# Twenty-five transposes of a two-layer encoder trunk, moved from TensorE to VectorE and a round trip through DRAM

## The chip, the cores and the metric

The kernel runs on one core of a Trainium2 chip. The metric is the device time of one execution in microseconds (us). Before the change the median of three runs is 2019.36 us (2019.31 to 2019.63).

## What is computed

Two layers act on x (256 tokens by 2048 channels, float32). Each layer normalises x and multiplies it by one wide matrix; the result feeds three token mixers and their gates. The outputs of the mixers are gated, projected to 2048 channels, scaled by sigmoid gates, summed, and sent through one more matrix into the residual. Cut to what matters here:

```python
h = _rmsnorm(x, g_pre)
u = h @ w_in                                       # 2048 -> 16192 columns
o_a = _mla_attention(qn, qr, kn, kr, v)            # A: low-rank q and kv
o_b = _rmsnorm(_diff_attention(bq, bk, bv, lam), b_g_sub) * (1.0 - lam_init)
cq = _rmsnorm(c_q.reshape(b, s, C_HEADS, C_DH), c_g_q)
ck = _rmsnorm(c_k.reshape(b, s, C_HEADS, C_DH), c_g_k)
o_c = _chunk_band_attention(cq, ck, cv, c_rel_bias)
branches = (o_a * silu(a_z), o_b * silu(b_z), o_c * silu(c_z))
y = sum(gates[:, :, n] * (branches[n] @ w_branch[n]) for n in range(3))
x = x + y @ w_out                                  # then the next layer
```

## The kernel before

All large products are weight streams. `matunit` computes a 256 x 512 block of a product (two PSUM tiles of 128 tokens) from chunks of weights: 256 rows by 512 columns, 512 KB each. For each chunk SyncE's queue loads it (L153, `_r`), ScalarE rounds it to float32r (L154, `_h`), VectorE forms the remainder (L155, `_l`), and TensorE runs twelve matmuls of 512 columns on it: two row blocks of the chunk, two token tiles, and three products each (high by high L163, remainder by high L164, high by low L165). Four chunks can be loaded ahead (`wrp`), three pairs can stand ready (`wsp`). A block over 2048 rows is a "unit" of 8 chunks, one over 1024 rows has 4.

A layer goes through its units in the order of `stream_plan`: cq, ckv and branch A; branch B in two halves of four heads (k, q, v, z); the first gate branch (n = 0: for each of four column blocks j one gate unit of 8 chunks and one branch unit of 4); branch C in two halves; the gate branches n = 1 and n = 2; the output projection in four column blocks (`l0o`), whose results are also the next layer's x.

Activations are computed with tokens on the partitions. The next product needs them with channels on the partitions. `to_transposed` (L199) does this: TensorE multiplies each 128 x 128 block by the identity (L205) into a PSUM tile, eight such transposes for 256 x 512 values, and ScalarE and VectorE split the tile into a high and a low part (`split`, L168, its lines L174 and L175). It is called for q and k of every branch, for z of A and C in `simple_half` (L352), for B's results in `b_split` (L546), for the four column blocks of y at the end of gate branch 2 (L639), and for the four column blocks of the next x (L702).

The code is written unit by unit. The order on each engine is made by a scheduler that runs the program through a model of time; each engine then works through its own list in order, and so does SyncE's queue of DMA issues.

Of the kernel before, what the change touches and what calls it, by code (L numbers as in the profile page):

```python
# [8 lines left out]
F32 = mybir.dt.float32  # L9
# [5 lines left out]
P = 128  # L15
# [6 lines left out]
HH = 4  # L22
# [20 lines left out]
def stream_plan():  # L43

    order = []
    for l in range(DEPTH):
# [35 lines left out]
def trunk_kernel(ctx: ExitStack, tc: tile.TileContext, x, xT, w, cols, rows, tab, bias, ident_d, out):  # L82
# [10 lines left out]
    natp = ctx.enter_context(tc.tile_pool(name="natp", bufs=6))  # L93
# [42 lines left out]
    state = {"off": 0}  # L136

    def matunit(lhs, K, N, name, pre=None):
# [3 lines left out]
        for c in range(nk // 2):  # L142
# [8 lines left out]
            for ks in ((slice(0, 1), slice(1, 2)) if o == 0 else (slice(0, 2),)):  # L151
                if o:
# [3 lines left out]
                                        op=ALU.subtract)  # L156
            for k2 in range(2):
# [56 lines left out]

    def rstd(ss, n, width, name):
# [4 lines left out]
    def qk_natural(ps, gs, rcol, name):  # L220

        ng = 512 // gs
        nats = [natp.tile([P, 512], F32, tag="nat", name=f"{name}_n{t}") for t in range(NT)]
# [19 lines left out]
        return nats  # L243
# [108 lines left out]
    def simple_half(z, parts, v, add, name):  # L352

        zt = zp.tile([P, HH, SEQ], F32, tag="z", name=f"{name}zt")
        to_transposed(lambda t: z[:, t, :], HH, None, None, None, f"{name}zT",
                      put=lambda bs, pt: nc.scalar.copy(zt[:, bs, :], pt))
        for hl in range(HH):
# [10 lines left out]
            nc.vector.tensor_tensor(out=zt[:, hl, :], in0=o[:, :SEQ], in1=zt[:, hl, :], op=ALU.mult)  # L368
# [39 lines left out]
    for l in range(DEPTH):  # L408
# [84 lines left out]
        ncq = []  # L493
        for t in range(NT):
# [4 lines left out]
            nat = natp.tile([P, 512], F32, tag="nat", name=f"ncq{l}{t}")  # L499
            nc.scalar.activation(nat, pcq[t], AF.Copy, scale=ss[:, t:t + 1])  # L500
            ncq.append(nat)
        abig = bigp.tile([P, 4, HH, SEQ], F32R, tag="big", name=f"abig{l}")
        cqh, cql = abig[:, 0], abig[:, 1]
        to_transposed(lambda t: ncq[t], 4, cqh, cql, lambda b: gcol(G_CQ + b), f"cqT{l}", per_block=True)
# [4 lines left out]
        nkv = []  # L509
        for t in range(NT):  # L510
# [9 lines left out]
            nat = natp.tile([P, 512], F32, tag="nat", name=f"nkv{l}{t}")  # L520
# [6 lines left out]
            nkv.append(nat)  # L527
# [18 lines left out]
        def b_split(z, hf, name, gain=None):  # L546
            bh[hf] = zp.tile([P, HH, SEQ], F32R, tag=f"bh{hf}", name=f"{name}h", bufs=1)
            bl[hf] = zp.tile([P, HH, SEQ], F32R, tag=f"bl{hf}", name=f"{name}l", bufs=1)
            if gain is None:
                split(bh[hf], bl[hf], z)  # L550
            else:
                to_transposed(lambda t: z[:, t, :], HH, bh[hf], bl[hf], gain, name)
# [229 lines left out]
```

## Time and profile before

| | |
|---|---|
| median of three runs | 2019.36 us |
| the profiled execution | 2019.73 us |
| its span, first to last instruction | 2018.0 us |
| granted TensorE clock, mean | 1.00 of full speed |
| TensorE busy | 2008.6 us, 100% |
| VectorE busy | 1228.0 us, 61% |
| ScalarE busy | 1117.8 us, 55% |
| moved by DMA | 377.37 MB, 187 GB/s over the span |

In the profile PE is TensorE, PEld its weight loads (they overlap with matmuls), DVE VectorE, ACT ScalarE, POOL GpSimd, SPq SyncE's queue of DMA issues. Names like `l0c0k` read as layer 0, branch C, half 0, k; `l0n2j1b` as layer 0, gate branch 2, column block 1, branch product; `l0g` are the gate units, `l0o` the output projection. L205 is line 205 of the kernel before. The chain of waits follows the instruction that ended last back to what released it at each step; an instruction in it lasts there from the end of the one before, not as long as its own record.

### The profile page before, as it was taken

To read this page: it belongs to the slowest core of one execution; us is meant where nothing else is said; L and a number is where in the kernel's file an instruction comes from. 1 tells how busy PE (TensorE), PEld (TensorE's weight loads), DVE (VectorE), ACT (ScalarE), POOL (GpSimd) and SP (SyncE) were. 2 spreads that over 40 slices of the span, in tenths; PEclk is the share of its full clock that TensorE was granted. 3 is DMA by queue.
4 is the path that set the end of the run, shared out by engine and by line. 5 is a ranking of instruction groups with operands and counts; after the bars stand their busy time and mean duration, and the time that the engine had idled before them with its cause. 6 is when DMAs were issued, how large, how long until landed. Compare 5 with 4: busy or idle time off the path is not lost.

```text
span 2018.0 us, 25748 instructions
## 1 busy us (share of the span) xinstructions
PE 2008.6 (100%) x9448; PEld 1676.6 (83%) x9448; DVE 1228.0 (61%) x1686; ACT 1117.8 (55%) x1658; POOL 218.6 (11%) x357
## 2 busy tenths in 40 slices
PE   9999999999999999999999999999999999999999
PEld 7888888888888888888888888888888888888887
DVE  5777878545555555555557778775455655555554
ACT  6666767445565544445456767674456555444443
POOL 2313040001000000000023130400010100000000
PEclk9999999999999999999999999999999999999999
DMA  8554545566555556557665445555665555565565
GB/s 288 185 165 151 175 165 184 180 206 193 185 170 184 173 193 194 191 186 242 208 191 181 157 157 176 168 169 189 206 199 178 167 187 175 192 196 189 188 240 156
DMA packets 107183, 377.37 MB, mean 187 GB/s; under 512 B 11937, under 2 KB 16033, under 8 KB 106289
## 3 DMA queue, kind: packets, MB, share of 16 engines
q1 hardware_dynamic: 104848, 366.75, 55.6%
q0 software_dynamic: 1920, 8.46, 1.4%
q8 instruction: 74, 1.21, 0.3%
q14 instruction: 53, 0.43, 0.1%
q10 hardware_dynamic: 288, 0.52, 0.1%
HBM read 371.49 MB, written 4.19 MB: 186 GB/s over the span
## 4 chain that ended last, share of the span: by engine, by line
PE 98%; DMA 1%; ACT 0%; DVE 0%; SPq 0%; issue 0%; ACTq 0%
PE l0g_p L164 4%; PE l1g_p L164 4%; PE l1g_p L165 4%; PE l0g_p L165 4%; PE l1g_p L163 4%; PE l0g_p L163 4%; PE l0o_p L163 1%; PE l0o_p L164 1%; PE l0o_p L165 1%; PE l1o_p L165 1%; PE l1o_p L163 1%; PE l1o_p L164 1%; DMA l0cq_r<-w 1%; PE l0az_p L164 1%; PE l0az_p L163 1%; PE l1az_p L164 1%
## 5 line engine op out<-in xcount | busy, mean ns | idle before, releaser
L155 DVE TENSOR_TENSOR l0g_l<-l0g_r,l0g_h 128x1024 fp32r<-128x1024 f32 x96 | 117.5, 1224 | 109.6 <-ACT l0g_h L154 109.6
L155 DVE TENSOR_TENSOR l1g_l<-l1g_r,l1g_h 128x1024 fp32r<-128x1024 f32 x96 | 117.5, 1225 | 109.6 <-ACT l1g_h L154 109.6
L154 ACT CAST l0g_h<-l0g_r 128x1024 fp32r<-128x1024 f32 x96 | 101.1, 1053 | 136.3 <-PE l0g_p L165 85.6
L154 ACT CAST l1g_h<-l1g_r 128x1024 fp32r<-128x1024 f32 x96 | 101.1, 1053 | 136.0 <-PE l1g_p L165 85.6
L164 PE MATMUL l1g_p<-l1g_l,xh 128*128 128x512 f32 x384 | 150.3, 391 | 0.0
L164 PE MATMUL l0g_p<-l0g_l,xh 128*128 128x512 f32 x384 | 150.3, 391 | 0.0
L165 PE MATMUL l1g_p<-l1g_h,xl 128*128 128x512 f32 x384 | 149.9, 390 | 0.0
L165 PE MATMUL l0g_p<-l0g_h,xl 128*128 128x512 f32 x384 | 149.9, 390 | 0.0
L163 PE MATMUL l0g_p<-l0g_h,xh 128*128 128x512 f32 x384 | 136.3, 391 | 0.0
L163 PE MATMUL l1g_p<-l1g_h,xh 128*128 128x512 f32 x384 | 136.3, 391 | 0.0
L163 PEld LDWEIGHTS l0g_p<-l0g_h,xh 128*128 128x128 f32 x384 | 72.0, 188 | 14.8
L164 PEld LDWEIGHTS l0g_p<-l0g_l,xh 128*128 128x128 f32 x384 | 72.1, 188 | 14.7
L164 PEld LDWEIGHTS l1g_p<-l1g_l,xh 128*128 128x128 f32 x384 | 72.1, 188 | 14.7
L163 PEld LDWEIGHTS l1g_p<-l1g_h,xh 128*128 128x128 f32 x384 | 72.0, 188 | 14.8
L165 PEld LDWEIGHTS l1g_p<-l1g_h,xl 128*128 128x128 f32 x384 | 72.1, 188 | 14.5
L165 PEld LDWEIGHTS l0g_p<-l0g_h,xl 128*128 128x128 f32 x384 | 72.1, 188 | 14.5
L155 DVE TENSOR_TENSOR l1o_l<-l1o_r,l1o_h 128x1024 fp32r<-128x1024 f32 x32 | 39.2, 1225 | 41.6 <-ACT l1o_h L154 41.6
L154 ACT CAST l1o_h<-l1o_r 128x1024 fp32r<-128x1024 f32 x32 | 33.8, 1055 | 53.2 <-PE l1o_p L165 48.2
L155 DVE TENSOR_TENSOR l0o_l<-l0o_r,l0o_h 128x1024 fp32r<-128x1024 f32 x32 | 39.2, 1225 | 36.1 <-ACT l0o_h L154 36.0
L154 ACT CAST l0o_h<-l0o_r 128x1024 fp32r<-128x1024 f32 x32 | 33.7, 1054 | 40.9 <-PE l0o_p L165 31.2
L680 POOL DMA_DIRECT2D xres<-xscr x1 | 0.8, 792 | 315.7 <-PE l1n2j3yT_t L205 315.7
L680 POOL DMA_DIRECT2D xres<-x x1 | 0.8, 784 | 315.7 <-PE l0n2j3yT_t L205 315.7
(1646 smaller groups left out, 5904.4 us busy)
## 6 DMA issues: line engine op xcount, KB each, us to landing
l0g_r<-w SPq DMA_DIRECT2D x96, 512.0 KB, 3.4
l1g_r<-w SPq DMA_DIRECT2D x96, 512.0 KB, 3.4
l0o_r<-w SPq DMA_DIRECT2D x32, 512.0 KB, 4.2
l1o_r<-w SPq DMA_DIRECT2D x32, 512.0 KB, 4.2
l0az_r<-w SPq DMA_DIRECT2D x16, 512.0 KB, 3.6
l1az_r<-w SPq DMA_DIRECT2D x16, 512.0 KB, 3.7
l0b0k_r<-w SPq DMA_DIRECT2D x8, 512.0 KB, 3.3
l0b0q_r<-w SPq DMA_DIRECT2D x8, 512.0 KB, 3.4
```

Of the source, the lines that this page charges most:

```text
L154: state["cast"] = nc.scalar.copy(wh[:, ks, :N], wr[:, ks, :N])
L155: nc.vector.tensor_tensor(out=wl[:, ks, :N], in0=wr[:, ks, :N], in1=wh[:, ks, :N].bitcast(F32), op=ALU.subtract)
L163: nc.tensor.matmul(ps[t][:, :N], h[:, ts], wh[:, k2, :N], start=first, stop=False)
L164: nc.tensor.matmul(ps[t][:, :N], h[:, ts], wl[:, k2, :N], start=False, stop=False)
L165: nc.tensor.matmul(ps[t][:, :N], lo[:, ts], wh[:, k2, :N], start=False, stop=last)
L680: nc.gpsimd.dma_start(xres, x_src.rearrange("(t p) d -> p t d", p=P))
```

## The change

For 25 of the blocks of 256 x 512 values `to_transposed` gives way to a new helper, `bounce`. VectorE transposes each 128 x 512 tile in squares of 32 x 32 (`nc.vector.transpose`, two instructions per block) into a tile `_tu`; SyncE's queue writes that tile to a scratch area in DRAM (`_scr`, 512 KB in runs of 2 KB); four more DMAs read it back with the squares in their transposed places, each 32 partitions of eight runs of 512 bytes. The read brings the values into the tile they came from, or into another one (`dst`). `from_bounced` then splits them from SBUF into high and low parts. The 25 are: in each layer k, q and z of both halves of C, the results of both halves of B, and y's column blocks 0 to 2; and once the next x's column blocks 0 to 2. Column block 3 of y and of x, all of A, and B's k and q stay with TensorE.

The steps of a trip are spaced by weight chunks: `later(n, fn)` runs `fn` when n more chunks have been issued, and `issue_after` keeps a write or a read behind that chunk's load on SyncE's queue and a split behind that chunk's cast on ScalarE. For C's k and q the write comes after 8, the read after 10, the two halves of the split after 12 and 13 chunks; for C's z 6 and 8; for B 28 and 30; for y 9, 11 and 13; for x 7, 9 and 11. In C the unit of z now comes before that of v. The two gate activations of a unit run with the second token tile first (`gates`). The tiles of normalised q and k are allocated as pairs (`natp`, 3 of twice the size where there were 6). The multiplication with C's gate reads and writes z in the order in which the trip left it (`bounced`, `as_bounced`).

```diff
-            for s in (1, 0, 2, 3):
+            for s in (1, 0, 3, 2):
                 win("c", qc + s * BW + hf * 512, 512)
...
-    natp = ctx.enter_context(tc.tile_pool(name="natp", bufs=6))
+    natp = ctx.enter_context(tc.tile_pool(name="natp", bufs=3))
...
-    state = {"off": 0}
+    state = {"off": 0, "n": 0}
+    due = []
+    away = set()
+    def later(n, fn):
+        due.append((state["n"] + n, fn))
+    def run_due():
+        state["n"] += 1
+        for x in [x for x in due if x[0] <= state["n"]]:
+            due.remove(x)
+            x[1]()
...
+            run_due()
...
+    def nat_pair(name):
+        return natp.tile([P, NT, 512], F32, tag="nat", name=name)
+    def bounce(src, name, at, then=None, dst=None):
+        turned = zp.tile([P, NT, 4, HH, 32], F32, tag="z", name=f"{name}_tu")
+        scr = dram.tile([NT, P, 4, 128], F32, name=f"{name}_scr")
+        for t in range(NT):
+            nc.vector.transpose(turned[:, t].rearrange("p j b c -> p b j c"), src[:, t, :])
+        dst = src if dst is None else dst
+        flat = dst.rearrange("p t f -> p (t f)")
+        away.add(name)
+        def write():
+            with tc.issue_after(state["last"].ins):
+                nc.sync.dma_start(scr.rearrange("t p j f -> p t (j f)"), turned.rearrange("p t j b c -> p t (j b c)"))
+        def read():
+            sv = scr.rearrange("t (i r) j f -> j r (t i) f", r=32)
+            with tc.issue_after(state["last"].ins):
+                for j in range(4):
+                    nc.sync.dma_start(flat[32 * j:32 * j + 32].rearrange("p (q f) -> p q f", f=128), sv[j])
+            if then is None:
+                away.remove(name)
+        def use(b0):
+            with tc.issue_after(state["cast"].ins):
+                then(flat, slice(b0, b0 + 2))
+            if b0:
+                away.remove(name)
+        later(at[0], write)
+        later(at[1], read)
+        if then is not None:
+            later(at[2], lambda: use(0))
+            later(at[2] + 1, lambda: use(2))
+        return flat
+    def bounced(z, b):
+        return z.rearrange("p (q b c) -> p q b c", b=HH, c=32)[:, :, b, :]
...
+    def as_bounced(d):
+        if len(d.shape) == 2:
+            return d.rearrange("p (q c) -> p q c", c=32)
+        return d.rearrange("p b (q c) -> p q b c", c=32)
+    def from_bounced(z, bs, dh, dl, gain):
+        if gain is None:
+            split(as_bounced(dh[:, bs, :]), as_bounced(dl[:, bs, :]), bounced(z, bs))
+        else:
+            one = not callable(gain)
+            if one:
+                nc.scalar.activation(as_bounced(dh[:, bs, :]), bounced(z, bs), AF.Copy, scale=gain)
+            for b in range(bs.start, bs.stop):
+                g = gain if one else gain(b)
+                h, lo, zb = as_bounced(dh[:, b, :]), as_bounced(dl[:, b, :]), bounced(z, b)
+                if not one:
+                    nc.scalar.activation(h, zb, AF.Copy, scale=g)
+                nc.vector.scalar_tensor_tensor(out=lo, in0=zb, scalar=g, in1=h.bitcast(F32),
+                                               op0=ALU.mult, op1=ALU.subtract)
...
+    def gates(z, ps, rcol, func):
+        i = nc.scalar.activation(z[:, 1, :], ps[1], func, scale=rcol[:, 1:2])
+        with tc.issue_after(i.ins):
+            nc.scalar.activation(z[:, 0, :], ps[0], func, scale=rcol[:, 0:1])
     def silu_gate(ps, rcol, name):
         z = zp.tile([P, NT, 512], F32, tag="z", name=name)
-        for t in range(NT):
-            nc.scalar.activation(z[:, t, :], ps[t], AF.Silu, scale=rcol[:, t:t + 1])
+        gates(z, ps, rcol, AF.Silu)
...
-    def simple_half(z, parts, v, add, name):
-        zt = zp.tile([P, HH, SEQ], F32, tag="z", name=f"{name}zt")
-        to_transposed(lambda t: z[:, t, :], HH, None, None, None, f"{name}zT",
-                      put=lambda bs, pt: nc.scalar.copy(zt[:, bs, :], pt))
+    def simple_half(zt, block, view, parts, v, add, name):
...
-            nc.vector.tensor_tensor(out=zt[:, hl, :], in0=o[:, :SEQ], in1=zt[:, hl, :], op=ALU.mult)
+            zc = block(hl)
+            nc.vector.tensor_tensor(out=zc, in0=view(o[:, :SEQ]), in1=zc, op=ALU.mult)
...
+            for b0 in (0, 2):
+                from_bounced(z, slice(b0, b0 + 2), bh[hf], bl[hf], gain)
...
+            zb[hf] = bounce(zb[hf], f"{n}bT", (28, 30))
...
-                    to_transposed(lambda t: yacc[:, t, js], 4, yh[j], yl[j], None, f"{nm}yT")
+                    if j < 3:
+                        yz = zp.tile([P, NT, 512], F32, tag="z", name=f"{nm}yz")
+                        bounce(yacc[:, :, js], f"{nm}yT", (9, 11, 13),
+                               lambda z, bs, yt=yt: from_bounced(z, bs, yt[:, 0], yt[:, 1], None), yz)
+                    else:
+                        to_transposed(lambda t: yacc[:, t, js], 4, yh[j], yl[j], None, f"{nm}yT")
...
-                to_transposed(lambda t: nat[t], HH, th[:, 0], th[:, 1], cg[:, 2:3] if i == 0 else gcol(G_CKH),
-                              f"{n}{nm}T")
+                bounce(nat, f"{n}{nm}T", (8, 10, 12), lambda z, bs, th=th, i=i: from_bounced(
+                    z, bs, th[:, 0], th[:, 1], cg[:, 2:3] if i == 0 else gcol(G_CKH)))
+            zc[hf] = bounce(silu_gate(in_unit(f"c{hf}z"), rcol, f"{n}z"), f"{n}zT", (6, 8))
...
-            zc[hf] = simple_half(zc[hf], cparts, v, cadd, n)
+            zc[hf] = simple_half(zc[hf], lambda hl: bounced(zc[hf], hl), as_bounced, cparts, v, cadd, n)
...
-                to_transposed(lambda t: xres[:, t, js], 4, xg_next[0][j], xg_next[1][j],
-                              lambda b: colt[:, l + 1, G_PRE + 4 * j + b:G_PRE + 4 * j + b + 1],
-                              f"x{l + 1}T{j}", per_block=True)
...
+                def gx(b, j=j, l=l):
+                    return colt[:, l + 1, G_PRE + 4 * j + b:G_PRE + 4 * j + b + 1]
+                if j < 3:
+                    bounce(xres[:, :, js], f"x{l + 1}T{j}", (7, 9, 11),
+                           lambda z, bs, j=j, gx=gx: from_bounced(z, bs, xg_next[0][j], xg_next[1][j], gx),
+                           nat_pair(f"x{l + 1}n{j}"))
+                else:
+                    to_transposed(lambda t: xres[:, t, js], 4, xg_next[0][j], xg_next[1][j], gx, f"x{l + 1}T{j}",
+                                  per_block=True)
```

What this makes of the order on the engines, at three places.

On TensorE at y's first column block (`l0n2j0yT`), while the next gate unit runs, the transposes stand between the matmuls of one chunk; first the rows of before:

```order
L163 MATMUL l0g_p_7197<-l0g_h_7236,xh_1_134 128x512 [waits Activation_49]
L163 MATMUL l0g_p_7198<-l0g_h_7236,xh_1_134 128x512
L205 MATMUL l0n2j0yT_t_7183<-ident,yacc_3466 128x128 [waits DVE_49,PE_49]
L205 MATMUL l0n2j0yT_t_7190<-ident,yacc_3466 128x128 [waits PE_49]
L205 MATMUL l0n2j0yT_t_7183<-ident,yacc_3466 128x128 [waits DVE_49]
L205 MATMUL l0n2j0yT_t_7183<-ident,yacc_3466 128x128 x2
L205 MATMUL l0n2j0yT_t_7190<-ident,yacc_3466 128x128 x3
L164 MATMUL l0g_p_7197<-l0g_l_7237,xh_1_134 128x512 [waits DVE_49]
```

The same place after the change, where only the matmuls of the gate unit are left:

```order
L176 MATMUL l0g_p_7175<-l0g_h_7214,xh_1_134 128x512 [waits Activation_49]
L176 MATMUL l0g_p_7176<-l0g_h_7214,xh_1_134 128x512
L177 MATMUL l0g_p_7175<-l0g_l_7215,xh_1_134 128x512 [waits DVE_49]
L178 MATMUL l0g_p_7175<-l0g_h_7214,xl_1_138 128x512
L177 MATMUL l0g_p_7176<-l0g_l_7215,xh_1_134 128x512
```

The eight transposes are gone and nothing stands in their place.

On SyncE's queue behind C's first k, in half 0 of layer 0, weight loads stand alone before the change:

```order
L153 DMA l0c0q_r_4696<-w 128x1024 [waits DMAHW2_49,DVE_49]
L153 DMA l0c0q_r_4714<-w 128x1024 [waits DMAHW3_49,DVE_49]
L153 DMA l0c0v_r_4768<-w 128x1024 [waits DMAHW4_49,DVE_49]
L153 DMA l0c0v_r_4786<-w 128x1024 [waits DMAHW5_49,DVE_49]
L153 DMA l0c0v_r_4804<-w 128x1024 [waits DMAHW6_49,DVE_49]
```

After it the write of the trip (L246) and its four reads (L252) stand among them:

```order
L165 DMA l0c0q_r_4694<-w 128x1024 [waits DMAHW5_49,DVE_49]
L165 DMA l0c0z_r_4738<-w 128x1024 [waits DMAHW6_49,DVE_49]
L246 DMA l0c0kT_scr<-l0c0kT_tu 128x2x512 [waits DVE_49]
L165 DMA l0c0z_r_4756<-w 128x1024 [waits DMAHW7_49,DVE_49]
L252 DMA l0c0k_n<-l0c0kT_scr 32x8x128 [waits DMAHW3_49,PE_49]
L252 DMA l0c0k_n<-l0c0kT_scr 32x8x128 x2
L252 DMA l0c0k_n<-l0c0kT_scr 32x8x128 [waits DMAHW0_49]
L165 DMA l0c0z_r_4778<-w 128x1024 [waits DMAHW1_49,DVE_49]
```

The first read waits for the semaphore of the write (DMAHW3), with one weight load between the two; the load of the third chunk of z stands behind the reads.

On VectorE in the unit after C's q, between the remainders of the weight chunks, the two splits of 512 columns read PSUM before the change:

```order
L155 TENSOR_TENSOR l0c0v_l_4824<-l0c0v_r_4822,l0c0v_h_4823 128x1024 [waits DMAHW3_49,Activation_49]
L240 TENSOR_TENSOR l0c0q_n_4733<-l0c0q_n_4733,l0c0q_ss 128x512 [waits Pool_49]
L155 TENSOR_TENSOR l0c0v_l_4842<-l0c0v_r_4840,l0c0v_h_4841 128x1024 [waits DMAHW4_49,Activation_49]
L155 TENSOR_TENSOR l0c0v_l_4860<-l0c0v_r_4858,l0c0v_h_4859 128x1024 [waits DMAHW5_49,Activation_49]
L175 SCALAR_TENSOR_TENSOR l0c0q<-l0c0qT_t_4752,cgain,l0c0q 128x512 [waits Activation_49]
L175 SCALAR_TENSOR_TENSOR l0c0q<-l0c0qT_t_4759,cgain,l0c0q 128x512 [waits Activation_49]
```

After it the splits of k, in four, and the transposes of q stand there:

```order
L167 TENSOR_TENSOR l0c0z_l_4798<-l0c0z_r_4796,l0c0z_h_4797 128x1024 [waits DMAHW2_49,Activation_49]
L292 SCALAR_TENSOR_TENSOR l0c0k<-l0c0k_n,colt,l0c0k 128x256 [waits DMAHW6_49,DMAHW5_49,DMAHW7_49,DMAHW0_49,Activation_49]
L292 SCALAR_TENSOR_TENSOR l0c0k<-l0c0k_n,colt,l0c0k 128x256
L239 STREAM_TRANSPOSE l0c0qT_tu<-l0c0q_n 128x4x4x32 [waits DVE_49]
L321 TENSOR_TENSOR l0c0q_n<-l0c0q_n,l0c0q_ss 128x512 [waits Pool_49]
L167 TENSOR_TENSOR l0c0z_l_4819<-l0c0z_r_4817,l0c0z_h_4818 128x1024 [waits DMAHW3_49,Activation_49]
L292 SCALAR_TENSOR_TENSOR l0c0k<-l0c0k_n,colt,l0c0k 128x256 [waits Activation_49]
L292 SCALAR_TENSOR_TENSOR l0c0k<-l0c0k_n,colt,l0c0k 128x256
L239 STREAM_TRANSPOSE l0c0qT_tu<-l0c0q_n 128x4x4x32 [waits DVE_49]
L167 TENSOR_TENSOR l0c0z_l_4840<-l0c0z_r_4838,l0c0z_h_4839 128x1024 [waits DMAHW4_49,Activation_49]
```

The first split of k waits for the four reads, and the remainder of the fifth chunk of z stands behind it.

## Rows read from the trace of the kernel before

**Rows 1.** The page's first section: busy us (share of the span) and instructions.
```profile
PE 2008.6 (100%) x9448; PEld 1676.6 (83%) x9448; DVE 1228.0 (61%) x1686; ACT 1117.8 (55%) x1658; POOL 218.6 (11%) x357
```
**Rows 2.** The page's slices: busy tenths of TensorE and its granted clock.
```profile
PE   9999999999999999999999999999999999999999
...
PEclk9999999999999999999999999999999999999999
```
**Rows 3.** The page's chain that ended last, by engine.
```profile
PE 98%; DMA 1%; ACT 0%; DVE 0%; SPq 0%; issue 0%; ACTq 0%
```
**Rows 4.** The waits view: who waited for whom, us, times, longest.
```profile
ACT l0g_h L154 <- PE l0g_p L165: 85.6, 52, 1.9
...
SPq L153 <- DVE l0g_l L155: 218.5, 90, 4.3
```
**Rows 5.** Instructions of line 205: ns min/median/max, first and last start.
```profile
L205 PE MATMUL x1T_t<-ident,xres x32: 272/273/273, 949.6 to 1018.7; 128*128 128x128 f32 x32
```
**Rows 6.** The chain around y's first transposes: start us, us, what.
```profile
827.06 0.46 PE l0g_p L163 x2
827.52 0.87 PE l0n2j0yT_t L205 x8
828.40 0.23 PE l0g_p L164
```
**Rows 7.** The chain where branch products of n1 and n2 begin.
```profile
712.82 0.45 PE l0n1j1b_p L163 x2
...
745.46 0.45 PE l0n1j2b_p L163 x2
...
778.10 0.45 PE l0n1j3b_p L163 x2
...
844.31 0.45 PE l0n2j1b_p L163 x2
...
877.88 0.45 PE l0n2j2b_p L163 x2
...
911.44 0.45 PE l0n2j3b_p L163 x2
```
**Rows 8.** The chain around the transposes of C's z.
```profile
562.32 0.22 PE l0c0zT_t L205 x2
562.54 0.23 PE l0c1k_p L165
562.77 0.66 PE l0c0zT_t L205 x6
```
**Rows 9.** Instructions of VectorE's lines 155, 240 and 175: mean ns, or min/median/max.
```profile
L155 DVE TENSOR_TENSOR l0g_l<-l0g_r,l0g_h 128x1024 fp32r<-128x1024 f32 x96 | 117.5, 1224 | 109.6 <-ACT l0g_h L154 109.6
...
L240 DVE TENSOR_TENSOR l0c0k_n<-l0c0k_n,l0c0k_ss x2: 684/688/693, 492.0 to 495.0; 128x512 f32<-128x512 f32 x2
...
L175 DVE SCALAR_TENSOR_TENSOR xl<-x1T_t,colt,xh x16: 474/477/485, 951.1 to 1022.1; 128x256 fp32r<-128x256 f32 x16
...
L175 DVE SCALAR_TENSOR_TENSOR l0c0k<-l0c0kT_t,colt,l0c0k x2: 741/746/750, 500.1 to 500.8; 128x512 fp32r<-128x512 f32 x2
```
**Rows 10.** Windows in gate branch n1 and in C: busy us (instructions), clock, DMA share, GB/s.
```profile
core 0: us, PE busy (x) PEld busy (x) DVE busy (x) ACT busy (x) POOL busy (x), PEclk, DMA share, GB/s
700.00:740.00 40.00, 40.00 (x178) 33.15 (x177) 20.69 (x19) 16.28 (x17) 0.00 (x0) 1.00 0.60 196
500.00:600.00 100.00, 100.00 (x478) 83.55 (x477) 59.26 (x85) 58.63 (x88) 7.28 (x12) 1.00 0.54 177
```
**Rows 11.** DMA from 1022 to 1038 us, kv weights: packets, MB, share.
```profile
DMA packets 1633, 1.98 MB, mean 124 GB/s; under 512 B 96, under 2 KB 1632, under 8 KB 1632
...
q1 hardware_dynamic: 1632, 1.97, 45.3%
```
**Rows 12.** DMA issues: count, KB each, median us to landing.
```profile
l0c0v_r<-w SPq DMA_DIRECT2D x8, 512.0 KB, 3.3
...
xscr<-xres POOLq DMA_DIRECT2D x4, 512.0 KB, 4.2
```
**Rows 13.** SyncE's issues of line 153: ns min/median/max; kv weights have 256 pieces.
```profile
L153 SPq DMA_DIRECT2D l0g_r<-w x96: 327/328/328, 314.2 to 893.9; - x96
...
L153 SPq DMA_DIRECT2D l0ckv_r<-w x8: 539/540/652, 18.1 to 34.2; - x8
```
**Rows 14.** Timeline of C's first v chunk: load, cast, remainder, first use.
```profile
496.88 20.02 SPq L153 DMA_DIRECT2D l0c0v_r<-w  x8
...
505.43 1.05 ACT L154 CAST l0c0v_h<-l0c0v_r 128x1024 fp32r<-128x1024 f32 x1 [1.67 <-PE l0c0q_p L165]
...
506.51 1.23 DVE L155 TENSOR_TENSOR l0c0v_l<-l0c0v_r,l0c0v_h 128x1024 fp32r<-128x1024 f32 x1 [1.50 <-ACT l0c0v_h L154]
...
511.12 0.39 PE L164 MATMUL l0c0v_p<-l0c0v_l,xh 128*128 128x512 f32 x1
```

More of the change, by code (lines that the diff above doesn't have):

```diff
@@ L222, in qk_natural @@
         ng = 512 // gs
-        nats = [natp.tile([P, 512], F32, tag="nat", name=f"{name}_n{t}") for t in range(NT)]
+        pair = nat_pair(f"{name}_n")
+        nats = [pair[:, t, :] for t in range(NT)]
         for t in range(NT):
@@ L242, in qk_natural @@
                                     in1=ss[:, t, :ng].unsqueeze(2).to_broadcast([P, ng, gs]), op=ALU.mult)
-        return nats
+        return pair
     def rope(dst, src, ctab, stab, ng, half, eng, name):
@@ L508, in trunk_kernel @@
         ss = sm.tile([P, NT, 2], F32, tag="sskv", name=f"sskv{l}")
-        nkv = []
+        kvpair = nat_pair(f"nkv{l}")
+        nkv = [kvpair[:, t, :] for t in range(NT)]
         for t in range(NT):
@@ L519, in trunk_kernel @@
                                     op=ALU.mult)
-            nat = natp.tile([P, 512], F32, tag="nat", name=f"nkv{l}{t}")
+            nat = nkv[t]
             nc.scalar.activation(nat[:, :256], pkv[t][:, :256], AF.Copy, scale=ss[:, t, 0:1])
@@ L546, in b_split @@
         def b_split(z, hf, name, gain=None):
-            bh[hf] = zp.tile([P, HH, SEQ], F32R, tag=f"bh{hf}", name=f"{name}h", bufs=1)
-            bl[hf] = zp.tile([P, HH, SEQ], F32R, tag=f"bl{hf}", name=f"{name}l", bufs=1)
-            if gain is None:
+            bh[hf] = zp.tile([P, HH, SEQ], F32R, tag=f"bh{hf}", name=f"bh{hf}", bufs=1)
+            bl[hf] = zp.tile([P, HH, SEQ], F32R, tag=f"bl{hf}", name=f"bl{hf}", bufs=1)
+            assert name is None or not [x for x in away if x.startswith(name)]
+            if name is None:
                 split(bh[hf], bl[hf], z)
-            else:
-                to_transposed(lambda t: z[:, t, :], HH, bh[hf], bl[hf], gain, name)
+                return
+            for b0 in (0, 2):
+                from_bounced(z, slice(b0, b0 + 2), bh[hf], bl[hf], gain)
         za = [None, None]
@@ L605, in trunk_kernel @@
                     put = lambda bs, pt: split_stacked(d[0][:, bs, :], d[1][:, bs, :], pt, cg[:, 1:2])
[L606 removed]
+                to_transposed(lambda t: nat[:, t, :], HH, None, None, None, f"{n}{nm}T", put=put)
                 op[nm] = d
@@ L626, in gate_branch @@
                 g = wk.tile([P, NT, 512], F32, tag="g", name=f"{nm}g")
-                for t in range(NT):
-                    nc.scalar.activation(g[:, t, :], pg[t], AF.Sigmoid, scale=rcol[:, t:t + 1])
+                gates(g, pg, rcol, AF.Sigmoid)
                 pb = matunit(lambda kt: (bh[kt // 4][:, kt % 4, :], bl[kt // 4][:, kt % 4, :]), BW, 512, f"{nm}b")
@@ L701, in trunk_kernel @@
                 xg_next[1][j] = xgp.tile([P, 4, SEQ], F32R, tag=f"xl{j}", name=f"xl{l + 1}_{j}")
-                to_transposed(lambda t: xres[:, t, js], 4, xg_next[0][j], xg_next[1][j],
-                              lambda b: colt[:, l + 1, G_PRE + 4 * j + b:G_PRE + 4 * j + b + 1],
-                              f"x{l + 1}T{j}", per_block=True)
+                def gx(b, j=j, l=l):
[7 more added lines that the diff above has]
+                                  per_block=True)
         if more:
             x_src = xscr
+    assert not due and not away
 def _pack(inputs):
```

36 lines of the change are left out of this document (18 added, 18 removed).

## The prediction

> **What bounds the kernel now.** I read the page's first section first. TensorE is busy in 2008.6 of the span's 2018.0 us, VectorE in 61% and ScalarE in 55% of it [rows 1]. A busy TensorE alone proves little, so the next question is whether it is held up. The slices show it at 9 throughout, at the full granted clock [rows 2], and the chain of waits that ended last is TensorE for 98% of the span, ScalarE and VectorE for 0% [rows 3]. The waits view says the same from the other side: ScalarE's weight casts wait for TensorE to give a buffer back, and SyncE's weight loads wait for VectorE to free theirs [rows 4]. So everything that feeds TensorE follows its pace. An instruction taken off TensorE shortens the program by its own step, as long as the feeders keep up at the new pace; one put on another engine costs nothing while that engine's lateness stays inside the lead that it has.
>
> **What a transpose costs there.** Its record lasts 272 ns [rows 5], but matmuls are pipelined, and the price is the step in the chain. Eight transposes in a row take 0.87 us [rows 6], that is 0.109 us each. A better price comes from two stretches that differ by them alone. In the second gate branch (n1) one column block of gate and branch product has no transposes, in the third (n2) it has eight. The starts of the branch product lie 32.64 us apart in n1 (712.82, 745.46, 778.10) and 33.57 and 33.56 us apart in n2 (844.31, 877.88, 911.44) [rows 7]. Eight transposes therefore cost 0.925 us: their own 0.87 and some 0.05 us at the seams with the matmuls. Where the eight are split as two and six, as in branch C, the steps are the same, 0.22 and 0.66 us [rows 8].
>
> **What goes.** Twenty-five blocks of eight: per layer six of C (k, q and z of two halves), two of B's results, three of y, and three of the next x once; 12 + 4 + 6 + 3 = 25, that is 200 transposes. 25 x 0.925 = 23.1 us. No matmul is added, and at those places TensorE's order is the same matmuls without the transposes.
>
> **What comes, and what hides it.** Each block becomes a round trip: two VectorE transposes, one write to DRAM and four reads on SyncE's queue, and splits that now read SBUF.
>
> VectorE. The trace shows none of its transposes. From below I take the time of nothing less than half of a 128x512 tensor_tensor from SBUF, 0.34 us, from above the 1.22 us of twice as many elements; the row nearest in size is 0.69 us [rows 9], which I take. 50 x 0.69 = 34 us. In the 12 blocks of C's k and q and of B two splits of 0.75 us become four of half the size at 0.48 us [rows 9], 12 x 0.42 = 5 us more. So 40 us (bounds 22 to 66) go onto an engine that idles for 790 us. In the densest stretch for it, C from 500 to 600 us, it is busy for 59 of 100 us [rows 10]; four or five trips there add some 8 us. Hidden. ScalarE loses the copies of z in C, two per half, and the order of its gate activations is turned round, the second row tile first; it is idle for 45% of the span, and I put both at nothing.
>
> DMA engines. A block of gate and branch product is 144 matmuls in 32.64 us, 0.2267 us each, and a weight chunk feeds twelve: 512 KB every 2.72 us. In the pure gate stretch the engines are busy 0.60 of the time at 196 GB/s [rows 10], so a chunk takes 1.6 us of all sixteen. The write has 2 KB pieces, 1.6 us by bytes. The reads have 1,024 pieces of 512 B. The smallest pieces on this queue that the trace shows are the 1,280 B rows of the kv weights: 1.97 MB in 1,536 such pieces (and 96 small packets) took 45.3% of 16 us [rows 11], 7.25 us, or 76 ns for a piece on one engine. So the reads take between 1.6 us (by bytes) and 1,024 x 76 ns / 16 = 4.8 us (a piece of 512 B as long as one of 1,280 B). I take 3 us. A trip then costs the engines 4.6 us (3.2 to 6.4). In C three trips fall on 32 chunks: 32 x 1.6 + 3 x 6.4 = 70 us of 87 even at the upper bound. Bandwidth is not the bound.
>
> SyncE's queue. This is where a wait is added. Each read must wait until its write has landed, and everything behind it on SyncE, the weight loads first of all, stands with it. The write stands one or two weight loads ahead of the read. A 512 KB store of the residual lands in 4.2 us and a weight load in 3.3 us [rows 12]. With one load between, SyncE stands for 4.2 - 2.7 = 1.5 us. A load of 256 pieces occupies it for 0.54 us against 0.33 us for 128 [rows 13], so the four reads take 2.2 us more. The next weight load, due 2.7 us after the last, goes out 1.0 us late and finds up to 4.8 - 2.2 = 2.6 us of reads ahead of it: 3.6 us late in all, and 5.2 us if the write first queues behind the 1.6 us of a weight chunk. Is that much? The first weight load of C's v was issued at 496.88, cast at 505.43, subtracted until 507.74 and first needed by TensorE at 511.12 [rows 14]. Landing in 3.3 us it lay 5.2 us before its cast, and the finished pair another 3.4 us before its matmul: 8.6 us of lead. Hidden, with 3 us to spare, and the lead is won back because the engines have 40% free.
>
> The Trainium skill (VectorE: DVE Perf Modes, The three transpose paths) warns that a plain DMA that transposes by access-pattern strides is 19 times slower than the crossbar's when the innermost destination stride is large. Here the innermost run is 512 B on both sides, and the 1,280 B pieces show nothing like it [rows 11]; taken at its word the warning would make a read 30 us (19 x 1.6, an estimate by that page) and the program far slower. The same page (Rules for kernel authors) sends a 128x128 transpose to TensorE when PSUM is a fit destination; by that rule alone the change loses, but it weighs engines one by one, and here TensorE is the one without idle time [rows 1, 3].
>
> **The sum.** The profiled execution took 2019.73 us, its span 2018.0 and 1.7 us around it; the median of the runs is 2019.36, 0.4 us less. 2019.36 - 23.1 = 1996.3 us. For small seams where a burst on VectorE or ScalarE delays a weight pair I add 0.7 us: 1997.0 us, 1.1% faster. The likeliest case's own range is 1994 to 2002.
>
> **The rivals.**
> *Part of the gain stays in new waits.* The splits of what was read stand in ScalarE's and VectorE's order between weight casts, and both engines work in order. If a read lands late, the split waits and the casts behind it wait too. The finished pair has 3.4 us of lead [rows 14], so a read must be over 3 us late at the split. For it: C has z's trip directly behind q's, and VectorE gets two splits, a transpose and a scaling within two chunks there. Against: a load goes out 8.55 us before its cast [rows 14], and the split stands two casts further on, so that after SyncE's 1.5 and 2.2 us the read has 8.55 + 5.44 - 3.7 = 10.3 us to land. If the 17 trips of C's k and q, y and x lose 0.6 us each, 10 us are gone: 2007 us (2002 to 2015).
>
> *No change.* TensorE would wait for pairs at the pace of its feeders. The pair needs 1.05 us on ScalarE and 1.23 us on VectorE in 2.72 us [rows 14], and neither chain nor waits show TensorE waiting for them [rows 3, 4], so little speaks for it: about 2019 us.
>
> *Slower: weights stuck behind the round trip.* The place is SyncE's queue at each of the 25 reads. The delay of the next weight load is (landing of the write - 2.7 + 2.2 - 2.7) plus (time of the reads - 2.2). It begins to cost at 8.6 us, and the change becomes a loss where it reaches 8.6 + 0.93 = 9.5 us. With writes that land in 4.2 us that needs reads of 10.7 us on the engines, 167 ns for a piece of 512 B; a weight piece of 4 KB takes 1.6 x 16 / 128 = 200 ns, one of 1,280 B takes 76 ns, so the trace leaves it possible but unlikely. At 200 ns a piece the reads take 12.8 us, the delay is 1.0 + 10.6 = 11.6 us, and the 25 trips lose 3.0 us each: 1996 + 75 = 2071 us.
>
> **Chances and range.** As forecast (below 2002 us) 0.73; part of the gain kept 0.14; no change 0.05; slower 0.08. A measurement of this kernel tells about 0.2%, 4 us, from no change: faster 0.86, same 0.06, slower 0.08. The range of 1993.5 to 2010 us begins 2.8 us below the sum, for seams that cost more than in n2, and reaches over most of the second case; what it leaves out is under 2 in 10.
>
> **What the profile after would show.** Right: 25 groups of transposes gone from the chain, the starts of the branch product in n2 32.64 us apart for j = 1 and 2, the chain still 98% TensorE, span near 1995, VectorE up by 22 to 66 us, no wait of TensorE for a weight pair in C. Wrong: rows in the waits view in which TensorE waits for VectorE's weight differences or a cast waits for a weight load; reads that land later than 8 us after their issue; a chain that passes through the round trip's DMAs; or distances in n2 that stay above 33 us.

## The result and the profile after

The changed kernel takes 1997.77 us (median of 4 runs, 1997.30 to 1998.21), the kernel before in the same comparison 2019.34. The ratio is 0.9893, with a 95% interval from 0.9876 to 0.9910: 1.1% faster, 0.8 us above the 1997.0 forecast. The profiled execution took 1997.89 us, its span 1996.1, 21.9 less than before.

The page's first section and its chain by engine, of the changed kernel:

```profile
PE 1985.4 (99%) x9248; PEld 1655.5 (83%) x9248; DVE 1257.8 (63%) x1764; ACT 1111.6 (56%) x1652; POOL 220.0 (11%) x357
...
PE 95%; POOL 1%; ACT 1%; DVE 1%; DMA 1%; issue 0%; SPq 0%; POOLq 0%; ACTq 0%
```

Against [rows 1], TensorE lost 200 instructions and 23.2 us of busy time. VectorE gained 29.8 us and lies at 63%. But the span fell by 21.9 us only, so TensorE is idle for 10.7 us where it was for 9.4, and the chain of waits leaves TensorE for 3% more of the span than in [rows 3]. Those 1.3 us will need an explanation.

First the price of a block. The chain, where the branch product begins in the third gate branch:

```profile
836.70 0.45 PE l0n2j1b_p L176 x2
...
869.34 0.45 PE l0n2j2b_p L176 x2
...
901.98 0.45 PE l0n2j3b_p L176 x2
```

They lie 32.64 us apart, the distance that n1 had and n2 had not [rows 7]. All 0.925 us of each block's eight transposes are gone there, and nothing took their place.

What came in their place lies elsewhere. VectorE's transposes (ns, min/median/max, first and last start):

```profile
L239 DVE STREAM_TRANSPOSE x1T_tu<-xres x6: 669/686/702, 936.6 to 980.4; 128x512 f32<-128x512 f32 x6
...
L239 DVE STREAM_TRANSPOSE l0c0kT_tu<-l0c0k_n x2: 706/706/707, 492.4 to 495.4; 128x512 f32<-128x512 f32 x2
```

SyncE's queue at the first trip of branch C (start us, us):

```profile
495.51 0.33 SPq L165 DMA_DIRECT2D l0c0z_r<-w  x1
496.14 0.38 SPq L246 DMA_DIRECT2D l0c0kT_scr<-l0c0kT_tu  x1
497.30 0.33 SPq L165 DMA_DIRECT2D l0c0z_r<-w  x1
500.88 2.87 SPq L252 DMA_DIRECT2D l0c0k_n<-l0c0kT_scr  x4
503.84 10.75 SPq L165 DMA_DIRECT2D l0c0z_r<-w  x6
```

The write goes out at 496.14, one weight load follows, and then SyncE stands until 500.88 for the write to land. The next weight load leaves at 503.84, where 497.30 + 2.72 = 500.02 was due: 3.8 us late. Reads land 4.9 us after their issue (2.7 at least, 7.9 at most), and the split of k waits for nothing: ScalarE does it at 512.24, in its turn.

The windows show where TensorE is idle (us, then busy us of TensorE, its weight loads, VectorE, ScalarE and GpSimd, each with its number of instructions, the granted clock, the DMA share and GB/s). In branch B's second half, first of layer 0 and then of layer 1, the kernel before had:

```profile
300.00:400.00 100.00, 100.00 (x478) 83.30 (x477) 67.29 (x119) 60.54 (x107) 6.43 (x13) 1.00 0.56 182
...
1200.00:1300.00 100.00, 100.00 (x484) 83.53 (x484) 75.70 (x133) 68.36 (x123) 20.45 (x34) 1.00 0.51 169
```

After the change these stretches, the one ahead of the first of them, and the stretch of C that [rows 10] shows read:

```profile
200.00:300.00 100.00, 100.00 (x484) 83.48 (x483) 76.88 (x136) 68.51 (x122) 23.42 (x39) 1.00 0.48 168
300.00:400.00 100.00, 99.55 (x471) 82.85 (x470) 69.60 (x123) 61.69 (x109) 6.45 (x14) 1.00 0.61 198
...
500.00:600.00 100.00, 100.00 (x467) 83.37 (x466) 62.68 (x94) 57.48 (x85) 7.27 (x12) 1.00 0.67 221
...
1200.00:1300.00 100.00, 99.55 (x478) 82.69 (x477) 78.93 (x137) 69.74 (x124) 24.09 (x40) 1.00 0.50 173
```

C, the place that I had feared for, has TensorE at 100.00 of 100, with VectorE 3.4 us busier. New idle time is in B: TensorE was busy for 99.55 us in each of its two stretches, where it had no gap before. The waits view names it, two new rows of TensorE waiting for VectorE's weight differences:

```profile
PE l0b1v_p L177 <- DVE l0b1v_l L167: 0.5, 1, 0.5
PE l1b1v_p L177 <- DVE l1b1v_l L167: 0.5, 1, 0.5
```

No round trip's read is near: this is the v unit of B's second half. VectorE's timeline shows what came in ahead of it, the transposes of B's first half (start us, us):

```profile
279.59 0.68 DVE L314 TENSOR_REDUCE l0b1k_ss<-l0b1k_sq 128x8 f32<-128x512 f32 x1
280.19 1.30 DVE L239 STREAM_TRANSPOSE l0b0bT_tu<-l0b0z 128x512 f32<-128x512 f32 x2
281.40 1.19 DVE L167 TENSOR_TENSOR l0b1v_l<-l0b1v_r,l0b1v_h 128x1024 fp32r<-128x1024 f32 x1
282.69 0.69 DVE L321 TENSOR_TENSOR l0b1k_n<-l0b1k_n,l0b1k_ss 128x512 f32<-128x512 f32 x1
```

The kernel before had the weight difference and the scaling of k there without them (in square brackets idle time of the engine just before, and what ended it):

```profile
280.36 1.22 DVE L155 TENSOR_TENSOR l0b1v_l<-l0b1v_r,l0b1v_h 128x1024 fp32r<-128x1024 f32 x1
281.95 0.69 DVE L240 TENSOR_TENSOR l0b1k_n<-l0b1k_n,l0b1k_ss 128x512 f32<-128x512 f32 x1 [0.38 <-POOL l0b1k_ss L238]
```

The transposes push both back by about a microsecond. GpSimd's rotation of k then ends later, and after it the rest of the chain up to TensorE: VectorE begins the weight difference that TensorE waits for at 300.63, where it began at 299.88. So the two waits seem to belong to the change, though not to its DMAs; four of the experiments test this. They make 0.9 us. Another 0.7 lie in the first 50 us, where no trip is (TensorE busy 45.42 us against 46.13; in the runs below those 50 us vary from 45.42 to 46.62), and the end has 0.4 less idle time than before.

### The profile page after: what moved, and what is told of

It reads as the page before. It is cut to its first block, busy times and chain, and to the rows that moved or that the text cites. A ratio compares the mean times of both kernels' runs of the same rounds, so it can differ in the third digit from the quotient of the medians.

```text
span 1996.1 us, 25598 instructions
## 1 busy us (share of the span) xinstructions
PE 1985.4 (99%) x9248; PEld 1655.5 (83%) x9248; DVE 1257.8 (63%) x1764; ACT 1111.6 (56%) x1652; POOL 220.0 (11%) x357
## 4 chain that ended last, share of the span: by engine, by line
PE 95%; POOL 1%; ACT 1%; DVE 1%; DMA 1%; issue 0%; SPq 0%; POOLq 0%; ACTq 0%
PE l0g_p L176 4%; PE l0g_p L178 4%; PE l1g_p L178 4%; PE l1g_p L177 4%; PE l1g_p L176 4%; PE l0g_p L177 4%; PE l0o_p L177 1%; PE l0o_p L178 1%; PE l0o_p L176 1%; PE l1o_p L177 1%; PE l1o_p L178 1%; PE l1o_p L176 1%; DMA l0cq_r<-w 1%; PE l0az_p L177 1%; PE l0az_p L176 1%; PE l1az_p L177 1%
```

## Experiments

The main theory: TensorE sets the pace, 0.925 us a block, and the round trips are covered. The rivals: the trips keep part of the gain; the other edits (z's unit ahead of v's in C, the gate's tiles in the other order, both row tiles in one tile) bring something by themselves. In the comparisons of these runs the kernel before had 2019.24 to 2019.44 us.

**The trip without its DMAs.**

```
-        later(at[0], write)          # and the four reads behind it
-        flat = dst.rearrange("p t f -> p (t f)")
+        flat = turned.rearrange("p t j b c -> p (t j b c)")
```

> The changed kernel without its 25 writes to DRAM and without their reads: the splits read the tile that VectorE has transposed in 32x32 squares, so the squares are not moved to their places (that part of the computation is left out). VectorE's transposes, the splits and the order of all else stay. Theory 1 (the trip is hidden, the gain is TensorE's time alone): 1997.8 us, within 0.5 us. Theory 2 (trips cost something through SyncE's queue or the DMA engines): lower; at 0.1 us a trip 1995.3 us. If the two new TensorE waits in branch B's second half came from the trips, they would go here too and give 0.9 us.

Measured 1998.61 us (1998.14 to 1999.62), ratio 0.9898 (0.9884 to 0.9912): not faster than with the trips. The two waits in B stayed (0.4 and 0.5 us of idle in the same windows). So 25 writes and 100 reads cost nothing that can be measured. The pages of this kernel and of the changed one also give the trips' price in engine time, by the queue that carries weights and trips (packets, MB, share of 16 engines), here without and then with them:

```profile
q1 hardware_dynamic: 104848, 366.75, 54.2%
```
```profile
q1 hardware_dynamic: 138848, 392.97, 58.9%
```

4.7% of 1996 us are 94 us, 3.75 us of all sixteen engines for each trip; I had taken 4.6 from bounds of 3.2 and 6.4. With the same traffic as in the first row the kernel before had 55.6%, and the one with nothing bounced (below) 53.7%; that spread is 1.5 us a trip, so the figure is a rough one.

**TensorE's transposes done as well.**

```
+        for b0 in (0, 2):
+            pt = ps_t.tile([P, 2, SEQ], F32, tag="t", name=f"{name}_t{b0}")
+            ... four nc.tensor.transpose for each block, pt not used
```

> The changed kernel, and the 200 TensorE transposes of the same 25 blocks done as well, their result unused. Theory 1 (TensorE sets the pace, a block of eight transposes is worth 0.925 us wherever it stands): 1997.8 + 25 x 0.925 = 2020.9 us. Theory 2 (part of the gain was lost to waits at the round trips, and a slower TensorE gives those back): less, some 2018 us, as 25 x 0.1 us of waits would be covered.

Measured 2020.56 us (11 runs, 2019.79 to 2021.06): 22.8 us more than the changed kernel, 0.91 us a block. Theory 2 wanted 2018. The trips ran in full beside the transposes, and the ratio to before is 1.0006 (0.9997 to 1.0015), so the whole gain is the transposes' time on TensorE. The two waits in B stay here too, as waits of 0.5 us of TensorE's transposes of k for GpSimd's rotation.

**Branch C back on TensorE.**

```
-                bounce(nat, f"{n}{nm}T", (8, 10, 12), ...)
+                to_transposed(lambda t: nat[:, t, :], HH, th[:, 0], th[:, 1], ...)
-            zc[hf] = bounce(silu_gate(...), f"{n}zT", (6, 8))
+            ... the same for z, with ScalarE's copy
```

> The changed kernel with the 12 blocks of branch C (k, q and z) back on TensorE, the 13 of y, of the next x and of branch B's results still by the round trip. Theory 1 (every block is worth the same, in whichever stage): 1997.8 + 12 x 0.925 = 2008.9 us. Theory 2 (C, the densest stretch for VectorE and with three trips close together, kept part of its gain): less than 2008.9, by what was kept; at a third of the gain 2005.2 us.

Measured 2009.20 us (5 runs, 2009.14 to 2009.69): 11.4 us more for 12 blocks, 0.95 us each. C gave its full share; a third of its gain kept would have been 2005.2.

**Nothing bounced, the other edits kept.**

> The changed kernel with no block by the round trip: all 25 transposed by TensorE. What stays of the change is the rest of its edits: z's unit ahead of v's in branch C, the gate's row tiles in the other order, and q and k of a unit in one tile of both row tiles. Theory 1 (those edits are worth nothing, but for the two waits of 0.45 us that TensorE has in branch B's second half): 2019.3 + 0.9 = 2020.2 us. Theory 2 (they gain by themselves): below 2019 us, by their share.

(The edit is that of the run before, for B's results, y and the next x too.) Measured 2020.00 us (11 runs, 2019.54 to 2020.87), ratio 1.0004 (0.9995 to 1.0012): the other edits bring nothing. The figure agrees with theory 1, but its reason for the 0.9 us was wrong. The two windows in B read:

```profile
300.00:400.00 100.00, 100.00 (x478) 83.45 (x477) 67.27 (x120) 60.53 (x108) 5.79 (x12) 1.00 0.54 182
1200.00:1300.00 100.00, 100.00 (x484) 83.50 (x484) 75.90 (x133) 68.46 (x123) 20.45 (x34) 1.00 0.49 169
```

Both row tiles of k lie in one tile here too, and TensorE waits nowhere in B. That takes the pair of tiles out as the cause, which I had suspected, and leaves what the trips put on VectorE.

**B's transposes later.** If they are the cause, moving these two alone must remove the waits.

```
+        def turn_late():
+            with tc.issue_after(state["sub"].ins):   # a given weight difference
+                turn()                               # the two vector.transpose
-            zb[hf] = bounce(zb[hf], f"{n}bT", (28, 30))
+            zb[hf] = bounce(zb[hf], f"{n}bT", (28, 30), turn_at=24 if hf == 0 else None)
```

> The changed kernel with VectorE's two transposes of branch B's first half (1.30 us, in both layers) moved behind the last weight difference of the next half's v unit; the write and the reads stay where they were. Theory 1 (these transposes stand ahead of the scaling of the next half's k, make it and GpSimd's rotation late, and so cause TensorE's two new waits of 0.45 us in the v unit): both waits go, 1997.8 - 0.9 = 1996.9 us. Theory 2 (the waits come from having both row tiles of k in one tile, or from elsewhere): they stay, 1997.8 us.

Measured 1998.21 us (1997.02 to 1998.67), by its time a miss. The waits view tells more than the time: TensorE's waits in the v unit are gone, and two others have come, at the first weights of the z unit:

```profile
PE l1b1z_p L177 <- DVE l1b1z_l L167: 0.4, 1, 0.4
PE l0b1z_p L177 <- DVE l0b1z_l L167: 0.4, 1, 0.4
```

The 1.30 us now stand ahead of z's first weight difference, in a stretch where VectorE is as dense with the splits of k. So these transposes do cause the waits, and the new place was badly chosen.

**B's transposes in a gap.** The same edit with `turn_at=21`.

> The changed kernel with VectorE's two transposes of branch B's first half, in both layers, put behind the fifth weight difference of the next half's v unit, into a stretch of 1.1 us in which VectorE idled there before the change. Behind the last weight difference they only moved TensorE's wait of 0.4 us to the first weights of the z unit. Theory 1 (VectorE's 1.30 us costs where VectorE has no idle time ahead of work that TensorE is about to need, and nothing where it has): both waits go and none comes, 1997.8 - 0.9 = 1996.9 us, and a span some 0.9 us under the changed kernel's 1996.1. Theory 2 (branch B's second half has no slack for them anywhere): a wait of 0.4 us at another row, 1997.8 us.

Measured 1996.33 us (1996.02 to 1997.52), ratio 0.9888 (0.9873 to 0.9902), the lowest median of this study. Its interval overlaps that of the changed kernel, so it is the trace and not the time that decides between the theories: the span is 1994.2, TensorE is at 100.00 us in both windows of B, the waits view has no row of TensorE in B, and the chain reads

```profile
PE 98%; DMA 1%; ACT 0%; DVE 0%; SPq 0%; issue 0%; ACTq 0%
```

as it did before the change [rows 3]. VectorE does the transposes at 288.69, between a weight difference and a reduction that it had been waiting for. Of the 1.9 us that the span fell the removed waits are 0.9; the rest is covered by the first 50 us, with 1.2 us less idle time (46.62 us busy against 45.42), which no edit touched.

**B's transposes twice**, in their place of the change.

```
-        for t in range(NT):
+        for t in (0, 1, 0, 1) if twice else (0, 1):
             nc.vector.transpose(...)
```

> The changed kernel with VectorE's two transposes of branch B's first half done twice in a row, in both layers: 1.30 us more on VectorE at that place, nothing else changed. Theory 1 (that place is where VectorE's time reaches TensorE): each of the two waits grows from 0.45 by up to 1.30 to 1.75 us, 1997.8 + 2.6 = 2000.4 us. Theory 2 (the waits have another cause, and VectorE's time is hidden there as elsewhere): 1997.8 us.

Measured 2003.68 us (2002.66 to 2006.26), 5.9 more than the changed kernel where 2.6 were expected and theory 2 wanted none. The place is the right one; the size was off, by a longer wait and by the clock. The second pair did not run in a row with the first: it came behind the weight difference (282.75 and 283.94), with the scaling of k between its two. And both of GpSimd's 128x8 multiplications there (281.65 and 284.57) took 1.25 us, where in the changed kernel one did (see the last section). The wait is now one of TensorE's own transposes of k for GpSimd's rotation, and it is longer than the 1.75 us of the sum:

```profile
PE l1b1kT_t L218 <- POOL l1b1k_n L339: 2.5, 1, 2.5
PE l0b1kT_t L218 <- POOL l0b1k_n L339: 2.5, 1, 2.5
```

That is 2 x (2.54 - 0.45) = 4.2 us. The rest is the clock: behind the wait of the first layer TensorE, busy in full for over 40 us until then, ran at a granted clock of 0.51 for a time, the lower of its two levels (1.2 and 2.4 GHz). The windows there (2 us each):

```profile
288.00:290.00 2.00, 0.32 (x3) 0.32 (x4) 1.31 (x2) 0.00 (x0) 1.84 (x3) 1.00 0.60 205
290.00:292.00 2.00, 2.00 (x8) 1.53 (x7) 0.00 (x0) 0.72 (x2) 1.17 (x4) 0.51 0.86 281
292.00:294.00 2.00, 2.00 (x7) 1.64 (x6) 1.30 (x2) 0.61 (x2) 1.11 (x2) 0.63 0.25 98
294.00:296.00 2.00, 2.00 (x10) 1.60 (x10) 0.89 (x1) 1.05 (x1) 1.84 (x4) 1.00 0.00 0
```

Eight steps of 0.425 us instead of 0.227 (289.87 to 293.27 in TensorE's timeline) cost 1.6 us; 4.2 + 1.6 is the difference of the two profiled spans, 5.8 us.

**The reads twice and three times.** How much lead does SyncE's queue have left?

```
-                for j in range(4):
+                for j in [j for _ in range(2) for j in range(4)]:   # and range(3)
                     nc.sync.dma_start(flat[32 * j:32 * j + 32]..., sv[j])
```

> The changed kernel with the four reads of every round trip done twice, the second four after the first have landed. SyncE then stands some 6.7 us longer in each of the 25 trips (1.8 us of issue and 4.9 us for landing). Theory 1 (SyncE's standing is covered by a lead of the weight loads of 8.6 us before the change; the trip uses 3.3 us and some issue of it, so that about 5 to 6.5 us are left): little is lost, 0 to 1.2 us in a trip, 1998 to 2028 us. Theory 2 (what SyncE stands is paid for): 1997.8 + 25 x 6.7 = 2165 us.

> The changed kernel with the four reads of every round trip done three times in a row, each four after the four before have landed: 13.4 us more of SyncE's standing in each of the 25 trips. Theory 1 (a lead of 8.6 us, beyond which every microsecond counts): with 5 to 6.5 us left, 6.9 to 8.4 us are lost in a trip, 2170 to 2208 us. Theory 2 (what SyncE stands is paid for): 1997.8 + 25 x 13.4 = 2333 us. If even this is hidden, there is more lead than the time from load to use shows: below 2010 us.

Measured 1998.61 us (1997.89 to 2001.15) for two and 2029.23 us (2025.62 to 2032.12) for three. Two lies at the low end of theory 1, three far below its 2170 us. SyncE's queue shows why (the kernel with three, the first two trips of C):

```profile
500.77 8.28 SPq L252 DMA_DIRECT2D l0c0k_n<-l0c0kT_scr  x12
509.09 8.66 SPq L165 DMA_DIRECT2D l0c0z_r<-w  x6
...
525.20 1.81 SPq L252 DMA_DIRECT2D l0c0q_n<-l0c0qT_scr  x4
527.11 0.39 SPq L165 DMA_DIRECT2D l0c0v_r<-w  x1
```

The edit did not do what both theories took for granted. Only in the four trips of C's k do the reads stand in a row; in the other 21 something else of the queue stands between some of the fours, as the weight load at 527.11 does (the next four reads follow at 529.97), and the same holds with the reads done twice. So most trips did not hold the weights back by the full amount, and the two totals say little about the lead. Where the reads do stand in a row, twelve took 8.28 us, not 2.87 + 13.4: each waits only for its own predecessor, which landed 2.6 us after its issue, and not for all four.

That first trip does measure the lead. The next weight load left at 509.09, where 497.37 + 2.72 = 500.09 was due, 9.0 us late, and TensorE waited half a microsecond for the remainder of this chunk, which puts the lead at 8.5 us:

```profile
PE l0c0z_p L177 <- DVE l0c0z_l L167: 0.5, 1, 0.5
```

Most of what three times cost is something else. Of the 34.3 us between the spans TensorE waited 20.0 and was busy 14.3 longer with the same instructions, at a mean clock of 0.994. The largest group of the waits, 13.0 us in four, is for the splits of what was read; the longest:

```profile
PE l1c_s L368 <- ACT l1c1q L286: 4.8, 1, 4.8
```

**SyncE standing, the reads in time.** Fifteen or thirty small copies behind each trip's reads, on which nothing depends, delay the weight loads and not the reads of their own trip.

```
+                for i in range(15):                      # and range(30)
+                    nc.sync.dma_start(aux[i:i + 1, :], scr[0, i:i + 1]...)
```

> The changed kernel with fifteen copies of 2 KB (DRAM to DRAM, unused) on SyncE's queue behind the four reads of each of the 25 trips: at 0.33 us of issue each SyncE stands 5.0 us longer ahead of the next weight load; the reads themselves are not later. In the changed kernel that load goes out 3.8 us late (503.84 for a load due 2.72 after 497.30). Theory 1 (the weights' lead is 8.6 us, as the times of load, cast and use gave): 3.8 + 5.0 - 8.6 = 0.2 us a trip, 1998 to 2005 us. Theory 2 (the lead is longer, and what cost when the reads were done three times over was only the late split of what was read): 1998 us, no wait for weights. Theory 3 (less lead is left than 5 us): at 2 us of lead left 75 us more, 2073 us.

> The changed kernel with thirty such copies of 2 KB behind the four reads of each trip: SyncE stands 10 us longer. Theory 1 (a lead of 8.6 us, and beyond it every microsecond counts): 3.8 + 10 - 8.6 = 5.2 us a trip, 1997.8 + 130 = 2128 us, TensorE waiting for weight differences behind the trips. Theory 2 (a longer lead): below 2050 us. Theory 3 (less lead): above 2150 us.

Measured 2080.85 us (2074.72 to 2084.58) and 2320.15 us (2317.33 to 2323.86). Read by theory 1's own figures both are too slow, but a copy behind others takes 0.62 us of the queue and not 0.33:

```profile
505.06 0.33 SPq L165 DMA_DIRECT2D l0c0z_r<-w  x1
508.71 2.09 SPq L252 DMA_DIRECT2D l0c0k_n<-l0c0kT_scr  x4
510.85 9.32 SPq L255 DMA_DIRECT2D l0c0kT_aux<-l0c0kT_scr  x15
520.27 7.89 SPq L165 DMA_DIRECT2D l0c0z_r<-w  x6
```

The load due at 505.06 + 2.72 = 507.78 went out at 520.27, 12.5 us late; with thirty it went out at 546.00, where 520.65 + 2.72 = 523.37 was due, 22.6 us late. TensorE's timeline behind this trip, first with fifteen and then with thirty:

```profile
524.83 0.84 PE L176 MATMUL l0c0z_p<-l0c0z_h,xh 128*128 128x512 f32 x2 [3.10 <-ACT l0c0z_h L166]
526.09 0.80 PE L177 MATMUL l0c0z_p<-l0c0z_l,xh 128*128 128x512 f32 x1 [0.42 <-DVE l0c0z_l L167]
```
```profile
550.32 1.22 PE L176 MATMUL l0c0z_p<-l0c0z_h,xh 128*128 128x512 f32 x2 [13.02 <-ACT l0c0z_h L166]
551.58 0.80 PE L177 MATMUL l0c0z_p<-l0c0z_l,xh 128*128 128x512 f32 x1
```

TensorE waits for the rounded chunk first, does two matmuls on it, and then needs the remainder. Without a wait the first matmul on the remainder would have begun two steps of 0.227 us after the two on the rounded chunk were due: at 521.73 + 0.45, and with thirty copies at 537.30 + 0.45. It began 3.9 and 13.8 us later. 12.5 - 3.9 = 8.6 and 22.6 - 13.8 = 8.8 us: with the 8.5 us of the twelve reads that is three delays and one lead, the 8.6 us of theory 1, and beyond it each microsecond is paid in full. Theories 2 and 3 (a much longer and a much shorter lead) are out.

The totals are less simple. Against the changed kernel's span TensorE waited 52.4 and 238.9 us more, 2.1 and 9.6 us a trip, so that the trip shown is one of the dearer ones. The other 34.3 and 81.6 us are longer busy time for the same instructions, at mean clocks of 0.988 and 0.935.

## Why the prediction was right

**What bounds the kernel, and what a block costs.** Right. 23.1 us were to leave TensorE, its busy time fell by 23.2, and the runs with all blocks and with C's alone put a block at 0.91 and 0.95 us against 0.925. That price came from two stretches of the old trace which differ by the transposes alone; by the record of one, 272 ns, it would have been 2.2 us a block.

**VectorE.** A transpose took 0.67 to 0.71 us where 0.69 was taken, and VectorE's load grew by 30 us (40 forecast, bounds 22 to 66; the sum added up records, but neighbouring ones overlap, so that two transposes of 0.67 to 0.70 us took 1.30 together). "Hidden" was right for 46 of the 50 and wrong for the four of B's first half (two in each layer): I had looked at C, the stretch that three trips share, and judged cover by an engine's busy share over 100 us. In B the share is higher (VectorE 76 to 79 us of 100), and the transposes stand just ahead of work that leads to TensorE.

**SyncE's queue.** Right in kind, off in its sizes. SyncE stands for 3.3 us before the reads (497.63 to 500.88; 1.5 forecast), because the write took longer than the 4.2 us that I had carried over from another store: landing had a median of 4.9 us, and up to 7.1. The reads took 2.87 us of issue there (2.2 forecast). The next weight load left 3.8 us late where 1.0 was forecast for its issue. The lead that covers this was put at 8.6 us, by taking landing and processing off the time from load to use, and three delays measured it at 8.5 to 8.8. The slower rival's mechanism exists and has its point of decision where it was said, but the trip shown stays 4.8 us away from it (8.6 - 3.8).

**The DMA engines.** About 3.75 us a trip instead of 4.6 (good to some 1.5 us), hidden in either case.

**The seams.** The 0.7 us that I added for weight pairs delayed by a burst on VectorE or ScalarE have a place: two waits of 0.45 us in B. The mechanism was named, the place was not, and my sign of it ("no wait of TensorE for a weight pair in C") looked at the wrong branch, while one of the signs of being wrong, rows of TensorE waiting for weight differences, did come, at 0.9 us in all. That 0.7 lies so near to 0.9 is luck: it was worked out from no row. A chain still 98% TensorE was wrong for the same reason: it reads 95%, and 98% once the two transposes are moved.

**The rivals.** "Part of the gain stays in new waits" is refuted as it was put, as late reads: without the trips' DMAs the time is no lower. The 0.9 us that did stay in waits come from VectorE's transposes. "No change" and "slower" did not come.

## What to carry to other kernels

On a kernel whose one engine has no idle time, price an instruction there by the distance of two stretches that differ by it alone, and price its replacement by the lead of whatever it delays: time from load to use, minus landing and processing. Here such a sum gave 8.6 us and the delays 8.5 to 8.8: a lead is worth all of its length and nothing beyond it. And look for cover not in an engine's busy share but in the rows just behind the place where the new instruction will stand; moving two transposes in each layer by eight microseconds removed waits of 0.9 us, as much as one more block taken off TensorE.

## What was not expected of the hardware

**GpSimd's small operations stretch beside VectorE.** The chain of the changed kernel runs through GpSimd there (start us, us):

```profile
281.12 0.21 POOL l0b1k_ss L297
...
281.39 1.26 POOL l0b1k_ss L319
```

The second, a 128x8 multiplication, takes 0.25 us a few rows further on (284.33 in GpSimd's timeline), and 0.21 and 0.20 us at this place in the kernel before and with the transposes in the gap, where no weight difference begins beside it. Here it begins at 281.39, beside the weight difference that VectorE began at 281.40, and ends just after it: 1.26 us. So a VectorE instruction that moves can lengthen work on GpSimd that does not depend on it, which is part of how 1.30 us reached TensorE. The Trainium skill (GPSIMD Engine Reference, Specifications) says that GpSimd shares its way to SBUF with VectorE and that an instruction of VectorE with two inputs in SBUF contends for it. The trace agrees: the weight difference has two.

**The same wait can cost the clock or not.** With the transposes doubled, TensorE waited 2.54 us in both layers. In the first the granted clock fell to 0.51 behind it; in the second, behind the same stretch of work, the window behind the wait shows

```profile
1284.00:1286.00 2.00, 1.76 (x9) 1.50 (x10) 0.00 (x0) 0.15 (x1) 1.66 (x5) 1.00 0.93 293
```

What decides it stays open. Over the whole span the mean clock was 0.994 with the reads three times and 0.935 with thirty copies, and TensorE was busy 14.3 and 81.6 us longer than in the changed kernel: waits cost more than their length there.
